# Seven-product pairs one slot later, and seven products in the last pass of a squared-ReLU MLP

## The chip, the cores and the metric

The kernel runs on one core of one Trainium2 chip. A core has a matmul engine (TensorE, PE in the profile, with its weight loads as PEld), three engines for elementwise work (VectorE or DVE, ScalarE or ACT, GpSimdE or POOL), an engine that issues DMAs (SyncE, SP), an on-chip memory of 128 partitions (SBUF), and eight banks of accumulators (PSUM) into which PE writes. The metric is the device time of one execution in microseconds, as the median of several runs. The kernel before took 2000.79 us, the median of 3 runs between 1999.85 and 2004.03.

## The reference, cut to what matters

A two-layer decoder trunk on 256 rows of width 2048, in float32. Layer 0 mixes with a short gated convolution, layer 1 with multi-head latent attention, and each layer ends in a squared-ReLU MLP with 8192 hidden columns. Every sublayer is followed by a normalisation of `ALPHA * h + f(h)`.

```
def sq_relu_mlp(x, w1, w2):
    return jnp.square(jax.nn.relu(x @ w1)) @ w2

for layer in range(DEPTH):                       # DEPTH = 2
    ...                                          # mix: convolution or attention
    h = layer_norm(ALPHA * h + mix, ln_g[layer, 0], ln_b[layer, 0])
    h = layer_norm(ALPHA * h + sq_relu_mlp(h, mlp_w1[layer], mlp_w2[layer]),
                   ln_g[layer, 1], ln_b[layer, 1])
```

x is 256 x 2048, w1 is 2048 x 8192 and w2 is 8192 x 2048 for each layer. The two MLPs take more than half of the time, and the change lies in them.

## The kernel before, in words

**Precision.** A float32 matrix is held as two parts, `hi` (rounded by a cast on ACT, L136) and `lo` (the rest, a subtraction on DVE, L137), and a product is built from two or three matmuls: hi times hi, hi times lo, lo times hi. The function `split` does both steps. `dot` (L309, L311, L312) issues the three matmuls of a 128 x 512 output, and the units of w1 use L224 and L228. Every weight is loaded from memory as a raw tile of 512 KB (`load_raw`, L147, on SP's queue) and split this way before PE can use it. Raw tiles and split tiles come from pools of fixed size, and weights are prepared in the order of one list, `stream`.

**The passes of an MLP.** The 8192 hidden columns are handled in NQ = 8 passes of QC = 8 chunks of 128 columns. For each chunk m of a pass a unit computes `x @ w1` for it: 32 matmuls into one PSUM bank, which `whole` evacuates with a copy on ACT (L366) and an addition on DVE (L367) into half of the tile `fp`. Two chunks share one `fp`, and the pool holds one of them. Relu and square follow on ACT (L732, in one case on DVE, L728).

Passes 0 and 7 multiply the activations by w2 in the ordinary way (`down`, or `down_late` for the last blocks): per output block of 512 columns and half of the rows, three matmuls for each chunk. Passes 1 to 6, called FAST, use a scheme of seven products in place of eight for a 2 x 2 split (`FACTORS`): from a pair of chunks `form` makes sums and differences of quarter tiles (L644 to L648), `split` makes hi and lo of them (tiles h1c, h1a, h3c, h3a), and `fast_products` issues seven dots, 21 matmuls, for one pair of chunks and one pair of output blocks (a group g). A pass has eight such products, numbered i = 0 to 7: four chunk pairs j by two groups. Their w2 tiles (`w2f`) need sums of weights as well, done on DVE (L171, L175, L178) between the casts.

**The sums of a group** lie in seven PSUM banks while the group is being worked on; the eighth bank, "unit", takes the units of w1. When the group is changed (after product i = 3 of a pass; two passes that follow one another take the groups in opposite order, so that none is due between them) the seven banks are copied to SBUF (`put_back`, L620) and those of the other group are copied in (`resume`, L693). After the last fast pass `fold` adds the seven sums to the output blocks (L628).

**Order.** `steps` yields for every pass q and slot m a unit and, from SHIFT = 5 slots behind it, the product that goes with it. So product i of a pass runs at slot i + 5: the first three in its own pass, the other five in the next. After the unit of each odd m, `finish_pair` forms and splits that pair; the first pair of a pass is split after the product of slot m = 1. [...]

**The end.** In the last MLP, `last_sum` copies output blocks into PSUM banks, the last pass's w2 is multiplied there, and `to_out` normalises each row half t: statistics per block (L1042), their aggregate (L1048), a correction by matmuls (L1071, L1076), and scaled outputs (L1059) stored to memory.

Of the kernel before, what the change touches and what calls it, by code (L numbers as in the profile page):

```python
# [11 lines left out]
F32R = mybir.dt.float32r  # L12
AF = mybir.ActivationFunctionType
# [3 lines left out]
P = 128  # L17
W = 256 + 2
T = 256
# [15 lines left out]
NB = 4  # L35
BW = D // NB
FAST = range(1, NQ - 1)
SHIFT = 5


def TURN(q, m, extra):
    return m == 0 or not (q == 1 and m < SHIFT or q == NQ - 1 and m > SHIFT) or extra and q == 1 and m <= NB
FIRST = (0, 1, 2, 3, 4, 6, 8, 12, 16)
LEAD = 4
HEAD = 4
# [11 lines left out]
def trunk(ctx: ExitStack, tc: tile.TileContext, xT, vecs, lead, w_first, w_in, w_out, w_kv, w_q, w_uk, w_uv,  # L57
# [21 lines left out]
    def halves(w):  # L79

        lead = len(w.shape) - 2
        return [(w,)] if lead == 0 else [h for i in range(w.shape[0]) for h in halves(w[i])]
# [6 lines left out]
    def steps():  # L89

        for q in range(1, NQ):
            for m in range(QC):
                p, i = (q, m - SHIFT) if m >= SHIFT else (q - 1, m + QC - SHIFT)
                yield q, m, (p, i // NB, i % NB, (p % 2) ^ (i // NB)) if p in FAST else None

    def mlp_stream(l):
        out = halves(w1[l, :QC]) + halves(w2[l, 0])
        for q, m, pair in steps():
            out += halves(w1[l, q * QC + m])
# [3 lines left out]
        return out + halves(w2[l, NQ - 1])  # L103

    stream += mlp_stream(0) + halves(w_kv) + halves(w_q)
    for g in range(4):
# [27 lines left out]
    def split(hi, lo, src):  # L134

        nc.scalar.copy(hi, src)  # L136
        nc.vector.tensor_tensor(lo, src, hi.bitcast(F32), ALU.subtract)  # L137
# [218 lines left out]
    def fast_products(ps, x, j, fresh, ready, onto=()):  # L356

        b, = take(1, 6)
        a = {n: [x[j // 2][:, j % 2, o, i * P:(i + 1) * P] for o in range(2)] for i, n in enumerate(LEFT)}
        for p, l, r in FACTORS:  # L360
            dot(ps[p], b[r], a[l], p in fresh, p in ready, onto=p in onto)

# [223 lines left out]
    def mlp(idx, ln, blocks, fast, begin=None, extra=None, last=False):  # L586
# [35 lines left out]
        def fold(g):  # L622
# [59 lines left out]
        factors = [act.tile([P, QC // 4, 2, 7 * P], F32R, tag=tag, name=f"h{idx}{tag}") for tag in ("c", "a2")]  # L682
        ps, onto, fresh = {}, set(), set()
        folds = iter(())

# [8 lines left out]
                onto.add(p)  # L694

        begun = {0: FAST[0], 1: FAST[0]}

        def products_of(p, i, j, g):
# [12 lines left out]
            if p == FAST[-1] and j == NB - 1:  # L711
                folds = chain(folds, fold(g))

        for q, m, pair in steps():
            lone = pair is None
            if q == FAST[0] and m == SHIFT:
                for o, _, _ in FACTORS:
                    resume(o, 1)
            w = take(2, 7)
            at = "6" if lone and m % 2 == 0 else "unit"  # L720
            un = psum("ps_u", bank[at])
            mm_run([(w, un)], xhl, 0, NC, NC, turned=TURNED if TURN(q, m, extra) else None)
            if m % 2 == 0:
                u = fast.tile([P, 8 * P], F32, tag="fp", name="fp")
            whole(un, u[:, (m % 2) * T:(m % 2 + 1) * T])
            late = q in FAST and m >= QC - 2
            if late and m % 2:
                nc.vector.scalar_tensor_tensor(u[:, T:2 * T], u[:, T:2 * T], 0.0, u[:, T:2 * T], ALU.max, ALU.mult)  # L728
            elif late or m % 2:
                for function in (AF.Relu, AF.Square):  # L730
                    at = u[:, :T] if late else u[:, :2 * T]
                    nc.scalar.activation(at, at, function)  # L732
            if m % 2 and (m > 1 or lone):
                finish_pair(m // 2, u)
            if extra and q == FAST[0] and m < NB:
                for t in range(2):
                    extra(block, m, t, spare[1 + (2 * m + t) % 3])
            if begin and q == FAST[0] and m < 4:
                if m % 2 == 0:
                    nc.gpsimd.dma_start(parked[:, 4 * m:4 * m + 8, :], held_x[0][:, 4 * m:4 * m + 8, :])  # L740
            if q == FAST[0] and m == SHIFT:
                sums = act.tile([P, 4, 2, BW], F32, tag="xres", name=f"sums{idx}")
            if q == NQ - 1:
                for _ in range(3 if m >= SHIFT else 2):
# [5 lines left out]
            if q == NQ - 1 and last and m >= QC - 2:  # L750
                for t in range(2):
                    last_sum(m - QC + 2, t, spare[2 * (m - QC + 2) + t])
# [273 lines left out]
    def to_out(block, finals, h):  # L1026
# [11 lines left out]
        def scratch(i):  # L1038
            return raws.tile([P, 1024], F32, tag="raw", name=f"u{i}")[:, :BW]

        def finished(n, t, ps):
            nc.vector.bn_stats(out=stats[:, t, n, :], in_=ps)  # L1042
            if n < NB - 1:
# [4 lines left out]
            nc.vector.bn_aggr(out=mv, in_=stats[:, t, :, :])  # L1048
            ve = small.tile([P, 2], F32, tag="ve", name="ve")[:, :1]
            nc.vector.tensor_scalar(ve, mv[:, 1:2], LN_EPS, None, ALU.add)  # L1050
            r = small.tile([P, 2], F32, tag="rr", name="rr")[:, :1]
            us = {}

            def centred(i):
                us[i] = scratch(i)
                nc.vector.scalar_tensor_tensor(us[i], finals[i, t], mv[:, 0:1], gbt[:, i, :BW], ALU.subtract, ALU.mult)

            def scaled(i, x, other, op=ALU.add):
                nc.vector.scalar_tensor_tensor(block(i, t), x, r, other, ALU.mult, op)  # L1059
                store(t, i)  # L1060

            if t == 0:
                rsqrt(r, ve)
                for i in range(NB):
# [5 lines left out]
            for i in range(n):  # L1070
                nc.tensor.matmul(finals[i, t], means, gbt[:, i, :BW], start=False, stop=i > 0, skip_group_check=True)  # L1071
# [4 lines left out]
            nc.tensor.matmul(finals[0, t], devs, gbt[:, 0, BW:], start=False, stop=True, skip_group_check=True)  # L1076
            scaled(n, us[n], gbt[:, n, BW:])
            for i in range(1, n):
                scaled(i, finals[i, t], gbt[:, i, BW:])
            nc.scalar.activation(block(0, t), finals[0, t], AF.Copy, scale=r)  # L1080
            store(t, 0)
# [102 lines left out]
```

## Time and profile before

The profiled execution took 2002.59 us, its span is 2000.7 us, and the mean granted clock of TensorE was 0.998.

| engine | busy, us | share of the span | instructions |
|---|---|---|---|
| PE (matmul) | 1988.5 | 99% | 11062 |
| DVE | 1720.3 | 86% | 2505 |
| ACT | 1289.0 | 64% | 1914 |
| POOL | 5.6 | 0% | 27 |

The page's groups for the work around the change are: the low parts of the weights (L137, 710 of 128 x 1024, 854.6 us), the casts of the weights (L136, 710, 732.5 us), and the units' matmuls (L224, 1792 of 512 columns, 621.2 us; L228, 1792 of 256 columns, 485.0 us).

A line of the timeline gives start and duration in microseconds, engine, line of the kernel, operation, output and inputs, and in brackets how long the engine was idle before it and what released it. A row of a table by stretch gives the span, the busy time of PE, PEld, DVE, ACT and POOL with instruction counts, the granted clock of PE, the DMA share and GB/s; a table asked for one engine has that engine alone.

### The profile page before, as it was taken

The numbers are of one execution on the slowest core, as the hardware profiler recorded it, in microseconds if no ns is written. First come the engines' busy times: TensorE is split into PE (matmuls) and PEld (weight loads), VectorE is DVE, ScalarE is ACT, GpSimd is POOL, SyncE is SP. The second block draws the span as 40 slices with busy tenths as digits, with TensorE's granted clock in tenths as the row PEclk, the third lists the DMA queues.
The fourth block names the chain that finished last, engine by engine and source line by source line (L and its number), as shares of the span: only waits on it lengthen the run. The fifth ranks groups of instructions, "written<-read, shape, count | busy, mean of one in ns | idle before, by whom it ended". The sixth has DMA issues, their size and how long they took to land.

```text
span 2000.7 us, 29698 instructions
## 1 busy us (share of the span) xinstructions
PE 1988.5 (99%) x11062; PEld 1732.5 (87%) x11062; DVE 1720.3 (86%) x2505; ACT 1289.0 (64%) x1914; POOL 5.6 (0%) x27
## 2 busy tenths in 40 slices
PE   9999999999999999999999999999999999999998
PEld 8888888988788888888889998898888888888886
DVE  8667667787899999999988988778889999999995
ACT  6444445586667777677756665558666776767772
POOL 0000000000000000000000000000000000000000
PEclk9999999999999999999999999999999999999999
DMA  9766666574565555665764643656456556565572
GB/s 339 213 190 189 189 189 190 182 238 143 180 215 191 200 194 196 210 205 204 246 223 153 184 144 106 211 182 196 140 194 216 170 203 216 180 212 197 205 267 96
DMA packets 107712, 390.00 MB, mean 195 GB/s; under 512 B 11952, under 2 KB 12720, under 8 KB 107056
## 3 DMA queue, kind: packets, MB, share of 16 engines
q1 hardware_dynamic: 106560, 383.79, 58.7%
q0 software_dynamic: 864, 4.19, 0.6%
q8 instruction: 86, 1.41, 0.3%
q14 instruction: 58, 0.48, 0.1%
q10 hardware_dynamic: 144, 0.13, 0.0%
HBM read 383.87 MB, written 4.19 MB: 194 GB/s over the span
## 4 chain that ended last, share of the span: by engine, by line
PE 95%; DMA 2%; DVE 1%; issue 1%; ACT 0%; SPq 0%; DVEq 0%; POOLq 0%; ACTq 0%
PE ps_u L224 20%; PE ps_l L224 13%; PE ps_u L228 10%; PE ps L312 7%; PE ps L311 7%; PE ps L309 7%; PE ps_l L228 7%; PE ps_d L312 2%; PE ps_d L309 2%; PE ps_d L311 2%; PE ps_w L258 2%; PE ps_w L257 2%; PE ps_w L256 2%; DMA raw<-in_w2f_dram 1%; PE ps_g L258 1%; PE ps_g L256 1%
## 5 line engine op out<-in xcount | busy, mean ns | idle before, releaser
L137 DVE TENSOR_TENSOR lo<-raw,hi 128x1024 fp32r<-128x1024 f32 x710 | 854.6, 1218 | 167.1 <-ACT hi L136 97.6
L136 ACT CAST hi<-raw 128x1024 fp32r<-128x1024 f32 x710 | 732.5, 1054 | 220.2 <-PE ps_l L224 102.2
L224 PE MATMUL ps_u<-xhl,hi 128*128 128x512 f32 x1792 | 621.2, 393 | 0.0
L228 PE MATMUL ps_u<-xhl,lo 128*128 128x256 f32 x1792 | 485.0, 280 | 0.0
L224 PEld LDWEIGHTS ps_u<-xhl,hi 128*128 128x128 f32 x1792 | 328.8, 187 | 67.5 <-DVE fp L367 0.9
L228 PEld LDWEIGHTS ps_u<-xhl,lo 128*128 128x128 f32 x1792 | 338.1, 189 | 12.9
L224 PE MATMUL ps_l<-xhl_a,hi 128*128 128x512 f32 x704 | 244.1, 393 | 0.0
L228 PE MATMUL ps_l<-xhl_a,lo 128*128 128x256 f32 x704 | 195.4, 279 | 0.0
L136 ACT CAST hi_t<-raw_t 128x1024 fp32r<-128x1024 f32 x96 | 101.5, 1057 | 120.4 <-DVE raw_t L171 115.4
L224 PEld LDWEIGHTS ps_l<-xhl_a,hi 128*128 128x128 f32 x704 | 132.1, 188 | 29.9
L228 PEld LDWEIGHTS ps_l<-xhl_a,lo 128*128 128x128 f32 x704 | 131.9, 188 | 0.2
L171 DVE TENSOR_TENSOR raw_t<-raw,raw 128x1024 f32<-128x1024 f32 x96 | 116.9, 1217 | 9.8 <-DMA raw<-in_w2f_dram 9.8
L137 DVE TENSOR_TENSOR lo_t<-raw_t,hi_t 128x1024 fp32r<-128x1024 f32 x96 | 116.9, 1218 | 2.1 <-ACT hi_t L136 1.7
L366 ACT COPY t<-ps_u 128x256 f32<-128x256 f32 x112 | 41.7, 372 | 95.0 <-PE ps_u L228 94.7
L224 PE MATMUL ps_l<-z,hi 128*128 128x512 f32 x240 | 82.4, 391 | 0.0
L258 PE MATMUL ps_w<-xd,hi 128*128 128x258 f32 x256 | 72.7, 284 | 0.0
L256 PE MATMUL ps_w<-xd,hi 128*128 128x258 f32 x256 | 72.3, 282 | 0.0
L257 PE MATMUL ps_w<-xd,lo 128*128 128x258 f32 x256 | 72.3, 282 | 0.0
L224 PE MATMUL ps_l<-oT,hi 128*128 128x512 f32 x208 | 71.3, 391 | 0.0
L732 ACT ACTIVATE fp<-fp 128x512 f32<-128x512 f32 (+1 forms) x112 | 65.9, 588 | 7.2 <-DVE fp L367 6.8
L178 DVE TENSOR_TENSOR raw<-raw 128x512 f32<-128x512 f32 x96 | 66.1, 688 | 2.0
L175 DVE TENSOR_TENSOR raw<-raw,raw_t 128x512 f32<-128x512 f32 x96 | 65.6, 683 | 0.8
(350 smaller groups left out, 3880.0 us busy)
## 6 DMA issues: line engine op xcount, KB each, us to landing
raw<-in_w_dram SPq DMA_DIRECT2D x320, 512.0 KB, 4.1
raw<-in_w2f_dram SPq DMA_DIRECT2D x192, 512.0 KB, 5.2
raw<-in_w_in_dram SPq DMA_DIRECT2D x88, 512.0 KB, 3.7
raw<-in_w_out_dram SPq DMA_DIRECT2D x32, 512.0 KB, 3.7
raw<-in_w_o_dram SPq DMA_DIRECT2D x32, 512.0 KB, 4.2
raw<-in_w_kv_dram SPq DMA_DIRECT2D x10, 512.0 KB, 4.6
raw<-in_w_q_dram SPq DMA_DIRECT2D x8, 512.0 KB, 4.0
raw<-in_w_uk_dram SPq DMA_DIRECT2D x8, 512.0 KB, 4.6
```

The costliest lines, as they stand in the source:

```text
L136: nc.scalar.copy(hi, src)
L137: nc.vector.tensor_tensor(lo, src, hi.bitcast(F32), ALU.subtract)
L171: nc.vector.tensor_tensor(t.rearrange(two, a=2), b12.unsqueeze(1).to_broadcast([P, 2, BW]), r1.rearrange(two, a=2), ALU.subtract)
L178: nc.vector.tensor_tensor(t4, b21, b12, ALU.subtract)
L224: nc.tensor.matmul(ps, w[blk // 8][0][:, blk % 8, :], x, start=first, stop=False)
L228: nc.tensor.matmul(ps[:, :T], w[blk // 8][1][:, blk % 8, :], x[:, :T], start=False, stop=last)
L256: nc.tensor.matmul(ps[:, :W], hi, x[k][:, :W], start=k == 0, stop=False)
L257: nc.tensor.matmul(ps[:, :W], lo, x[k][:, :W], start=False, stop=False)
L258: nc.tensor.matmul(ps[:, :W], hi, x[k][:, W:], start=False, stop=k == NC - 1)
L309: nc.tensor.matmul(ps, x[0], w[0], start=first, stop=False, skip_group_check=onto)
L311: nc.tensor.matmul(ps[:, at], x[0], w[1][:, at], start=False, stop=False, skip_group_check=onto)
L312: nc.tensor.matmul(ps, x[1], w[0], start=False, stop=last, skip_group_check=onto)
```

## The change

- SHIFT goes from 5 to 6: every product runs one slot later behind the units, so two products of a pass run in its own pass and six in the next. Pass 1 has one more slot with a unit alone.
- The first two pairs of a pass are split after the products of slots 2 and 3 (dictionary `rows`), where they were split after the product of slot 1 and after the unit of slot 3.
- In the last MLP, `steps` goes on past the last pass. Two of the four output blocks (group 1, blocks 2 and 3) take the last pass's w2 by four times seven products, two of them in slots 6 and 7 and two behind the units. For that the last pass forms and splits all four pairs. `put_back` is then called for four of the seven sums, and `fold_last` folds the sums into three PSUM banks and one output block; blocks 0 and 1 keep the ordinary way. The order of blocks in `to_out` becomes 2, 3, 0, 1.
- In the first MLP's last pass the late units are split one by one.
- The factor tiles are 8 quarter tiles wide (7 before); `TURN` loses its clause on `extra`, which ran some units of the last MLP's pass 1 with their matmuls in another order (`TURNED`).

```
-SHIFT = 5
+SHIFT = 6
...
-def TURN(q, m, extra):
-    return m == 0 or not (...) or extra and q == 1 and m <= NB
+def TURN(q, m):
+    return m == 0 or not (q == 1 and m < SHIFT or q == NQ - 1 and m > SHIFT)
...
-        for q in range(1, NQ):
-            for m in range(QC):
+        for q in range(1, NQ + 1):
+            for m in range(QC if q < NQ else SHIFT):
...
+        def fold_last(g):
+            s1, s5, s7, s6 = (sums[:, i, g, :] for i in range(4))
+            left, right = 2 * g, 2 * g + 1
+            finals.update({(left, 1): ps["2"], (right, 1): ps["3"], (left, 0): ps["4"], (right, 0): block(right, 0)})
+            for d, a, b in ((ps["2"], ps["2"], s1), (s6, s6, s1), (ps["3"], ps["3"], s6), (s7, s7, s6),
+                            (ps["4"], ps["4"], s7), (block(right, 0), block(right, 0), s7), (ps["3"], ps["3"], s5),
+                            (block(right, 0), block(right, 0), s5)):
+                nc.vector.tensor_tensor(d, a, b, ALU.add)
...
-            if q in FAST:
+            if q in FAST or last:
                 form(u)
-                split(f[:, 0, :], f[:, 1, :], u[:, P:])
+                at = slice(P if q in FAST else 0, 8 * P)
+                split(f[:, 0, at], f[:, 1, at], u[:, at])
...
-            end = i == 0 or p == FAST[-1]
+            end = i == 0 or p == FAST[-1] and not last
...
                 for o in order:
+                    if p == NQ - 1:
+                        if o in OWN:
+                            put_back(o, g, ps[o])
+                        continue
...
-            late = q in FAST and m >= QC - 2
+            late = m >= QC - 2
...
-            if m % 2 and (m > 1 or lone):
-                finish_pair(m // 2, u)
+            if late and q not in FAST and not last:
+                f, at = factors[m // 4][:, 1], slice(m % 2 * T, (m % 2 + 1) * T)
+                split(f[:, 0, at], f[:, 1, at], u[:, at])
+            else:
+                rows[m // 2] = u
+            if m % 2 and (m > 3 or lone) and m // 2 in rows:
+                finish_pair(m // 2, rows.pop(m // 2))
...
-            if m == 1 and not lone:
-                finish_pair(0, u)
+            if m in (2, 3) and not lone:
+                finish_pair(m - 2, rows.pop(m - 2))
...
-            for i, (n, t) in enumerate(((2, 0), (3, 0), (2, 1), (3, 1))):
-                last_sum(n, t, spare[4 + i])
-            blocks(block, finals, h)
+            for n, t, o in ((0, 0, "unit"), (1, 0, "1"), (0, 1, "5"), (1, 1, "7")):
+                last_sum(n, t, bank[o])
+            blocks(block, finals, h, lambda: fold_last(1))
...
+        order = (2, 3, 0, 1)
...
-        for n in range(2):
-            down(h, finished, n, finals)
-        down_late(h, finished, range(2, NB), finals)
+        fold_last()
+        for n in order[:2]:
+            for t in range(2):
+                finished(n, t, finals[n, t])
+        down_late(h, finished, order[2:], finals)
```

More of the change, by code (lines that the diff above doesn't have):

```diff
@@ L37 @@
 FAST = range(1, NQ - 1)
-SHIFT = 5
-def TURN(q, m, extra):
-    return m == 0 or not (q == 1 and m < SHIFT or q == NQ - 1 and m > SHIFT) or extra and q == 1 and m <= NB
+SHIFT = 6
+def TURN(q, m):
+    return m == 0 or not (q == 1 and m < SHIFT or q == NQ - 1 and m > SHIFT)
 FIRST = (0, 1, 2, 3, 4, 6, 8, 12, 16)
@@ L87, in trunk, with steps @@
     stream += halves(w_out)
-    def steps():
-        for q in range(1, NQ):
-            for m in range(QC):
+    def steps(last):
+        for q in range(1, NQ + 1):
+            for m in range(QC if q < NQ else SHIFT):
                 p, i = (q, m - SHIFT) if m >= SHIFT else (q - 1, m + QC - SHIFT)
-                yield q, m, (p, i // NB, i % NB, (p % 2) ^ (i // NB)) if p in FAST else None
+                pair = (p, i // NB, i % NB, (p % 2) ^ (i // NB)) if p in FAST or last and p == NQ - 1 and i < NB else None
+                if q < NQ or pair:
+                    yield q, m, pair
     def mlp_stream(l):
         out = halves(w1[l, :QC]) + halves(w2[l, 0])
-        for q, m, pair in steps():
-            out += halves(w1[l, q * QC + m])
+        for q, m, pair in steps(l == 1):
+            if q < NQ:
+                out += halves(w1[l, q * QC + m])
             if pair:
@@ L102, in mlp_stream @@
                 out.append((w2f[l, p, g, j, 0], w2f[l, p, g, j, 1]))
-        return out + halves(w2[l, NQ - 1])
+        return out + halves(w2[l, NQ - 1, :2] if l else w2[l, NQ - 1])
     stream += mlp_stream(0) + halves(w_kv) + halves(w_q)
@@ L358, in fast_products @@
         b, = take(1, 6)
-        a = {n: [x[j // 2][:, j % 2, o, i * P:(i + 1) * P] for o in range(2)] for i, n in enumerate(LEFT)}
+        a = {n: [x[j // 2][:, j % 2, o, i * P:(i + 1) * P] for o in range(2)] for i, n in enumerate(LEFT, 1)}
         for p, l, r in FACTORS:
@@ L681, in mlp @@
         spare = [bank[p] for p in ("3", "1", "5", "7", "2", "4", "6", "unit")]
-        factors = [act.tile([P, QC // 4, 2, 7 * P], F32R, tag=tag, name=f"h{idx}{tag}") for tag in ("c", "a2")]
+        factors = [act.tile([P, QC // 4, 2, 8 * P], F32R, tag=tag, name=f"h{idx}{tag}") for tag in ("c", "a2")]
         ps, onto, fresh = {}, set(), set()
@@ L696, in mlp @@
         begun = {0: FAST[0], 1: FAST[0]}
+        rows = {}
         def products_of(p, i, j, g):
@@ L710, in products_of @@
                         resume(o, 1 - g)
-            if p == FAST[-1] and j == NB - 1:
+            if p == FAST[-1] and j == NB - 1 and end:
                 folds = chain(folds, fold(g))
-        for q, m, pair in steps():
+        for q, m, pair in steps(last):
             lone = pair is None
+            if q == NQ:
+                products_of(*pair)
+                continue
             if q == FAST[0] and m == SHIFT:
@@ L719, in mlp @@
             w = take(2, 7)
-            at = "6" if lone and m % 2 == 0 else "unit"
+            at = "6" if lone and (m - SHIFT) % 2 else "unit"
             un = psum("ps_u", bank[at])
-            mm_run([(w, un)], xhl, 0, NC, NC, turned=TURNED if TURN(q, m, extra) else None)
+            mm_run([(w, un)], xhl, 0, NC, NC, turned=TURNED if TURN(q, m) else None)
             if m % 2 == 0:
@@ L743, in mlp @@
             if q == NQ - 1:
-                for _ in range(3 if m >= SHIFT else 2):
+                for _ in range(3 if m >= SHIFT else 2 if not last or m > 2 else 0):
                     next(folds, None)
@@ L747, in mlp @@
                 products_of(*pair)
-            if m == 1 and not lone:
-                finish_pair(0, u)
-            if q == NQ - 1 and last and m >= QC - 2:
-                for t in range(2):
-                    last_sum(m - QC + 2, t, spare[2 * (m - QC + 2) + t])
+            if m in (2, 3) and not lone:
+                finish_pair(m - 2, rows.pop(m - 2))
         for _ in folds:
@@ L1024, in turn_residual, with to_out @@
         nc.vector.scalar_tensor_tensor(block(n, t), ps, ALPHA, block(n, t), ALU.mult, ALU.add)
-    def to_out(block, finals, h):
+    def to_out(block, finals, h, fold_last):
         gbt = act.tile([P, NB, 2 * BW], F32, tag="b", name="gbt")
@@ L1039, in scratch @@
             return raws.tile([P, 1024], F32, tag="raw", name=f"u{i}")[:, :BW]
+        order = (2, 3, 0, 1)
         def finished(n, t, ps):
             nc.vector.bn_stats(out=stats[:, t, n, :], in_=ps)
-            if n < NB - 1:
+            if n != order[-1]:
                 if t == 1:
@@ L1063, in finished @@
                 rsqrt(r, ve)
-                for i in range(NB):
+                for i in order:
                     centred(i)
@@ L1069, in finished @@
             nc.scalar.activation(means, negative, AF.Copy, scale=mv[:, 0:1])
-            for i in range(n):
-                nc.tensor.matmul(finals[i, t], means, gbt[:, i, :BW], start=False, stop=i > 0, skip_group_check=True)
+            one = order[0]
+            for i in order[:-1]:
+                nc.tensor.matmul(finals[i, t], means, gbt[:, i, :BW], start=False, stop=i != one, skip_group_check=True)
             rsqrt(r, ve, lambda: centred(n))
@@ L1075, in finished @@
             nc.scalar.activation(devs, id_t, AF.Copy, scale=ve)
-            nc.tensor.matmul(finals[0, t], devs, gbt[:, 0, BW:], start=False, stop=True, skip_group_check=True)
+            nc.tensor.matmul(finals[one, t], devs, gbt[:, one, BW:], start=False, stop=True, skip_group_check=True)
             scaled(n, us[n], gbt[:, n, BW:])
-            for i in range(1, n):
+            for i in order[1:-1]:
                 scaled(i, finals[i, t], gbt[:, i, BW:])
-            nc.scalar.activation(block(0, t), finals[0, t], AF.Copy, scale=r)
-            store(t, 0)
-        for n in range(2):
-            down(h, finished, n, finals)
-        down_late(h, finished, range(2, NB), finals)
+            nc.scalar.activation(block(one, t), finals[one, t], AF.Copy, scale=r)
+            store(t, one)
+        fold_last()
[3 more added lines that the diff above has]
+        down_late(h, finished, order[2:], finals)
     with tc.tile_pool(name="fast2", bufs=1) as fast:
```

## The prediction

> **What bounds the kernel now.** I read the page first, for the engine that ends last; then tables by stretch around the steps that the diff moves; then the timeline of single instructions there.
>
> ```profile
> PE 1988.5 (99%) x11062; PEld 1732.5 (87%) x11062; DVE 1720.3 (86%) x2505; ACT 1289.0 (64%) x1914; POOL 5.6 (0%) x27
> PE 95%; DMA 2%; DVE 1%; issue 1%; ACT 0%; SPq 0%; DVEq 0%; POOLq 0%; ACTq 0%
> ```
>
> TensorE holds 95% of the chain that ended last: time falls only where it has fewer matmuls or fewer waits. VectorE at 86% is a mean. In the steps of the seven-product passes it is full (table by stretch, last MLP, next to the last pass):
>
> ```profile
> 1900.80:1911.10 10.30, 10.30 (x56) 8.72 (x55) 10.30 (x14) 6.80 (x11) 0.00 (x0) 1.00 0.70 226
> 1911.10:1922.00 10.90, 10.90 (x58) 9.27 (x57) 10.90 (x15) 7.25 (x11) 0.00 (x0) 1.00 0.57 194
> ```
>
> After the span stand PE, PEld, DVE, ACT, POOL, the granted clock and DMA. PE and DVE are both busy throughout, so a stall of one soon becomes one of the other. PE's few stalls sit in the first seven-product pass of each MLP (product i=3):
>
> ```profile
> 501.57:511.94 10.37, 10.37 (x54) 8.74 (x53) 8.40 (x11) 6.66 (x9) 0.00 (x0) 1.00 0.49 155
> 511.94:518.48 6.54, 5.81 (x33) 4.80 (x32) 6.07 (x9) 1.55 (x3) 0.00 (x0) 1.00 0.87 308
> 518.48:528.53 10.05, 7.87 (x22) 5.91 (x23) 6.03 (x7) 6.67 (x11) 0.00 (x0) 0.66 0.45 147
> 528.53:538.95 10.42, 10.42 (x55) 8.84 (x54) 8.74 (x10) 10.09 (x15) 0.00 (x0) 1.00 0.42 125
> 1468.39:1474.57 6.18, 5.09 (x23) 3.86 (x22) 5.25 (x7) 4.32 (x9) 0.00 (x0) 1.00 0.50 139
> 1947.40:1990.95 43.55, 43.55 (x194) 1.00 0.32 112
> 1884.55:1889.35 4.80, 4.80 (x23) 1.00 0.61 227
> ```
>
> The first and fourth rows are undisturbed steps of 10.37 us: one W1 unit and one product. A product is 4.80 (last row, 21 matmuls, 0.2286 each), so a unit is 5.57. The stretches between are one unit (6.54) and one product (10.05); 1468.39 is a product of the last MLP. The row of 43.55 is the ordinary output of the last pass, 192 matmuls, 0.2268 each.
>
> ```profile
> 512.84 0.42 DVE L728 SCALAR_TENSOR_TENSOR fp<-fp 128x256 f32<-128x256 f32 x1
> ...
> 514.32 0.28 DVE L645 TENSOR_TENSOR fp<-fp 128x128 f32<-128x128 f32 x1
> ...
> 519.11 1.22 DVE L171 TENSOR_TENSOR raw_t<-raw,raw 128x1024 f32<-128x1024 f32 x1 [1.10 <-DMA raw<-in_w2f_dram]
> 520.26 1.08 DVE L137 TENSOR_TENSOR h1a<-fp,h1a 128x896 fp32r<-128x896 f32 x1
> ```
>
> ```profile
> 518.48 0.50 PE L309 MATMUL ps<-hi,h1a 128*128 128x512 f32 x1 [0.73 <-ACT h1a L136]
> ...
> 521.39 0.79 PE L312 MATMUL ps<-hi,h1a 128*128 128x512 f32 x1 [2.18 <-DVE h1a L137]
> 521.99 0.63 PE L309 MATMUL ps<-hi,h1a 128*128 128x512 f32 x1
> 522.41 0.63 PE L311 MATMUL ps<-lo,h1a 128*128 128x512 f32 x1
> 1471.03 0.73 PE L312 MATMUL ps<-hi,h3a 128*128 128x512 f32 x2 [1.09 <-DVE h3a L137]
> 1011.82 0.50 PE L312 MATMUL ps_d<-hi,h1a 128*128 128x512 f32 x1 [1.20 <-DVE h1a L137]
> ```
>
> Of the DVE rows three belong to the last pair of activations (relu, a small add, the low part of the split at 520.26), and one, ahead of that split, waited for weights, and PE waits for that pair (h1a, h3a). After 0.73 and 2.18 matmuls follow at 0.42 (521.99 to 522.41) instead of 0.23, with the clock at 0.66 over the stretch: of the 6.2 us lost there, 2.9 are waits and 3.3 the slower clock. After 1.09 the clock stayed 1.00.
>
> **What the change takes away.** (1) With SHIFT 6 product i=3 runs one step, 10.37 us, later, more than any of these waits. First MLP: (6.54−5.57)+(10.05−4.80) = 6.22 us. Last MLP: 6.18−4.80 = 1.38. What is late next is the same split one product on, with 10.37−2.9, some 7 us, to spare; if that cover goes, the price is what it is now. (2) At the first MLP's end the wait of 1.20, with the slow matmul beside it (0.50 for 0.39) 1.3, goes: late units are split by halves, and the split stands earlier on DVE's queue. (3) The last MLP's last pass computes two of its four output blocks by seven products: 84 matmuls for 96, so 96×0.2268+84×0.2286 = 40.98 for 43.55, a gain of 2.57. Together 11.5.
>
> DMA issues on SP's queue are as many as before, each product's weights one unit later in the stream and one unit later needed; POOL's queue is not touched. The longer factor tiles and their wider split (1024 for 896 columns, four pairs in the last pass) cost DVE and ACT 0.1 each; I put 0.4 in sum, range 0 to 0.6. Fewer turned units in the last MLP: ±0.3, taken as 0.
>
> **What it adds, first: the change of group (after product i=3, now in slot m=1) and the two slots behind it.** The activations of m=0 and 1 lie in one buffer, fp (one copy). They are now split after the product at m=2, where before it was after that at m=1. So the evacuation of unit m=2, which writes the next fp, must stand behind that split, the split behind product i=4, which still reads the factors it overwrites, and unit m=3 behind the evacuation, since all units of a pass use one PSUM bank. [...] Both queues around this place in the trace (last MLP, ACT then DVE):
>
> ```profile
> 1884.79 0.37 ACT L366 COPY t<-ps_u 128x256 f32<-128x256 f32 x1 [2.40 <-PE ps_u L228]
> 1886.11 0.59 ACT L693 COPY ps<-acc 128x512 f32<-128x512 f32 x1
> 1886.64 0.58 ACT L620 COPY sums<-ps 128x512 f32<-128x512 f32 x1
> 1887.12 1.05 ACT L136 CAST hi_t<-raw_t 128x1024 fp32r<-128x1024 f32 x1
> 1888.06 1.06 ACT L136 CAST hi<-raw 128x1024 fp32r<-128x1024 f32 x1
> ...
> 1901.04 0.64 ACT L732 ACTIVATE fp<-fp 128x512 f32<-128x512 f32 x1
> 1901.58 1.04 ACT L136 CAST hi<-raw 128x1024 fp32r<-128x1024 f32 x1
> ```
>
> ```profile
> 1888.20 1.23 DVE L137 TENSOR_TENSOR lo_t<-raw_t,hi_t 128x1024 fp32r<-128x1024 f32 x1 [0.24 <-ACT hi_t L136]
> 1889.35 1.22 DVE L137 TENSOR_TENSOR lo<-raw,hi 128x1024 fp32r<-128x1024 f32 x1
> 1890.48 0.68 DVE L137 TENSOR_TENSOR t<-raw,t 128x512 fp32r<-128x512 f32 x1
> 1891.08 1.22 DVE L137 TENSOR_TENSOR lo<-raw,hi 128x1024 fp32r<-128x1024 f32 x1
> ...
> 1900.59 0.42 DVE L367 TENSOR_TENSOR fp<-ps_u,t 128x256 f32<-128x256 f32 x1
> ```
>
> Start to start, on ACT: copies 0.48 and 0.53 (0.50), cast 0.95, activation 0.54; on DVE 1024 columns 1.14, 512 columns 0.60; the evacuation lasts 0.42. Count from the end of unit m=1. On ACT the new order has a copy, the first put-back and reload (their sum is ready after 3 matmuls, both done at 2.0), three casts (2.85), two activations (1.08) and a half cast (0.5): 6.5. Then twelve copies of 0.50: 12.5. Then a cast of 1.05: 13.5. Only then can DVE begin, and it goes on without a break: four of 1024 (4.56), one of 512 (0.60), one of 1024 (1.14), the split of the fp (1.0), one of 512 (0.60) and the evacuation (0.42): 8.3, so 21.8. PE has until then the product of m=1, unit m=2, the product of m=2, the next product and two matmuls: 4.80+5.57+4.80+4.80+0.46 = 20.4. It waits 1.4. Between PE and this chain there is no other work: in steady steps DVE is full. Eight such places (q=4 to 7, two MLPs): 11.2. Lower end 0: copies and casts overlap better than their order says. Upper end 1.9: 0.5 more where a weight cast lands before the copies. I take 1.4, since both ends come from the same rows and the sum of pitches lies nearer the upper one.
>
> Queued behind the waiting evacuation on DVE are the low parts of the next weights; behind ACT's cast of the fp, the casts of the next product. Either delays the product after. [...]
>
> **Second: the last pass.** Its product i=3 follows the last unit with only 18 matmuls and one product between: 18×0.2286+4.80 = 8.9 us. Behind that unit stand on DVE, durations less the 0.08 by which neighbours overlap: copy and evacuation (0.37+0.42), three of 512 (1.8), a relu of 256 (0.34), four of 1024 (4.56), adds of 128, 256 and 128 (0.20+0.34+0.20), 8.25, and a fourth 512 (0.6): 8.85. Then ACT, whose cast already under way has 0.9 left, casts the activations (1.05): 10.8. PE waits 1.9; 1.1 if the cast under way went behind, 2.2 with semaphores.
>
> **Third: the tail.** In the built order four scaled outputs of the first row half stand on DVE between the last statistics and their aggregate, where now they run before the last matmul:
>
> ```profile
> 1984.56 2.74 DVE L1059 SCALAR_TENSOR_TENSOR acc<-u,rr,gbt 128x512 f32<-128x512 f32 x4
> ...
> 1991.32 0.70 DVE L1042 BATCH_NORM_STATS2 stats<-ps_e 128x6 f32<-128x512 f32 x1 [2.81 <-PE ps_e L312]
> 1992.05 0.26 DVE L1048 BATCH_NORM_AGGREGATE mv<-stats 128x2 f32<-128x24 f32 x1
> ```
>
> Four take 2.74 less the 0.08 of overlap; nothing covers them there: 2.65. Lower end 0, if the last weights come sooner than the order supposes and the statistics end late; I take 2.65.
>
> **Sum.** −11.5+11.2+1.9+2.65+0.4 = +4.65. The profiled execution took 2002.59 us (span 2000.7); the median of the runs is 2000.79, 1.8 lower, within the runs' own scatter (1999.85 to 2004.03). I start between the two, at 2001.5, and forecast 2006.0 (rounded down). What a measurement of this kernel can tell from no change is 0.2%, 4.0 us: 1996.8 to 2004.8.
>
> **Rivals.** (a) *The swap is covered*, because put-backs and casts come earlier on the chip than pitches along the order make them: waits 0. −11.5+1.9+2.65+0.4 = −6.55: 1994.9, with the tail's lower end 1992.3. For it: the trace shows no PE wait in the change of groups before (1884 to 1905). Against: DVE is full there, and between the two products there is now no unit. It decides below a wait of (11.5−4.7−4.95)/8 = 0.23 a place, 4.7 being the way from 2001.5 to 1996.8. 0.18.
> (b) *Half covered.* Waits of 0.9 a place, 7.2: +0.65, 2002.1, no change. 0.24.
> (c) *The clock.* Where waits add up as at 518 to 521, the slow clock takes up to 3.3 more; at three of the eight changes of group +9.9: 2016.0. Against: the single waits of 1.09 and 1.20 cost one slow matmul at most. 0.10. [...]
> (d) *The stall stays.* If product i=3 of the first MLP comes as late again, 6.2 return: 2012.3. For it: at 519.11 the split stood behind weights that came 1.10 late. Against: 10.37 us more room. 0.08.
>
> **How the numbers follow.** The forecast has 0.40; with (c) and (d) slower has 0.58, same 0.24 from (b), faster 0.18 from (a). The range 1996 to 2013 leaves out most of (a) and the worse part of (c), some 0.2; the forecast's own is 2003 to 2010, by waits of 1.0 to 1.9.
>
> **What would show it.** Right: product i=3 in the first fast pass back to 4.80 at clock 1.00; a PE wait of 1 to 2 us near each change of group in q=4 to 7, released by the evacuation or a cast; 1.9 before the last pass's product i=3; aggregate 2.7 later than the last statistics. Wrong: no PE idle at the changes of group, or a clock under 1.00 there.

## The result, and the profile after

The changed kernel takes 2012.9 us (median of 4 runs, 2012.58 to 2014.15) against 2000.6 of the kernel before: a ratio of 1.0061, with a 95% interval of 1.0045 to 1.0077. It is slower by some 12 us. Its profiled execution took 2012.86 us with a span of 2011.0.

From the page of the changed kernel, its busy times and the chain that ended last:

```profile
PE 1991.4 (99%) x11050; PEld 1726.9 (86%) x11050; DVE 1748.0 (87%) x2540; ACT 1289.4 (64%) x1916; POOL 5.7 (0%) x27
PE 76%; DVE 11%; ACT 10%; issue 3%; DMA 1%; DVEq 0%; ACTq 0%
```

PE has 12 matmuls fewer, is busy 2.9 us longer, and its part of the chain fell from 95% to 76%: VectorE and ScalarE now release it. The summary of PE's waits (what it waited for, total us, times, longest) for the two stretches that hold the MLPs' passes, first MLP and then last:

```profile
PE ps_u L227 <- DVE fp L370: 1.7, 2, 1.0
PE ps L312 <- ACT hi L139: 1.2, 3, 0.5
PE ps L312 <- ACT t L139: 0.9, 2, 0.5
PE ps L314 <- DVE t L140: 0.5, 1, 0.5
...
PE ps L312 <- ACT hi L139: 1.8, 4, 0.5
PE ps L312 <- ACT h3a L139: 1.7, 1, 1.7
PE ps L312 <- ACT t L139: 1.5, 3, 0.5
PE ps_u L227 <- DVE fp L370: 0.8, 1, 0.8
```

The waits for the splits h1a and h3a in the first fast passes, which the prediction showed, are gone; the evacuation (fp), the casts (hi, t) and the low parts (t) are what PE waits for now. Product i=3 of the first fast pass takes 4.80 us at clock 1.00 (21 matmuls; the row counts a neighbour at each end with them):

```profile
522.40:527.20 4.80, 4.80 (x23) 3.95 (x22) 4.32 (x6) 3.88 (x7) 0.00 (x0) 1.00 0.42 130
```

One change of group, PE's timeline and then DVE's (last MLP, q=6):

```profile
1828.31 0.40 PE L315 MATMUL ps<-hi,h3c 128*128 128x512 f32 x1
1829.19 0.50 PE L312 MATMUL ps<-t,h3c 128*128 128x512 f32 x1 [0.48 <-ACT t L139]
1830.14 0.73 PE L312 MATMUL ps<-hi,h3a 128*128 128x512 f32 x2 [0.45 <-ACT hi L139]
1830.83 0.50 PE L314 MATMUL ps<-t,h3c 128*128 128x512 f32 x1
1831.16 0.40 PE L315 MATMUL ps<-t,h3c 128*128 128x512 f32 x1
1831.40 0.39 PE L227 MATMUL ps_u<-xhl,hi 128*128 128x512 f32 x1
```

```profile
1822.79 2.36 DVE L140 TENSOR_TENSOR lo<-raw,hi 128x1024 fp32r<-128x1024 f32 x2 [3.22 <-ACT hi L139]
1825.07 1.22 DVE L140 TENSOR_TENSOR lo_t<-raw_t,hi_t 128x1024 fp32r<-128x1024 f32 x1
1826.21 1.22 DVE L140 TENSOR_TENSOR lo<-raw,hi 128x1024 fp32r<-128x1024 f32 x1
1827.35 0.68 DVE L181 TENSOR_TENSOR raw<-raw 128x512 f32<-128x512 f32 x1
1827.95 1.22 DVE L140 TENSOR_TENSOR lo<-raw,hi 128x1024 fp32r<-128x1024 f32 x1
1829.08 1.08 DVE L140 TENSOR_TENSOR h3c<-fp,h3c 128x896 fp32r<-128x896 f32 x1
1830.09 0.69 DVE L140 TENSOR_TENSOR t<-raw,t 128x512 fp32r<-128x512 f32 x1
1830.69 0.42 DVE L370 TENSOR_TENSOR fp<-ps_u,t 128x256 f32<-128x256 f32 x1
```

DVE's row is the predicted one, instruction for instruction: it begins after 3.22 us of waiting for ACT and takes 8.3 us without a break, 1822.79 to 1831.11. PE meets the chain a little ahead of the evacuation: its two waits end with casts of the next weights on ACT (t and hi), and when unit m=3 begins at 1831.40 the evacuation is just over. PE's seven starts span 3.09 us for six matmuls that take 1.37 at 0.229: 1.72 are lost. Measured this way (start to start, above the pace of the matmuls), the first MLP loses 0.93 (q=2), 0.80 (q=4), 1.66, 1.69 and 2.39 (q=7), the last one 1.04, 0.99, 1.69, 1.72 and 1.85 at the same places: 14.8 us. At q=3 nothing is lost.

The last pass and the tail, PE and then DVE:

```profile
1969.65 0.50 PE L312 MATMUL ps<-hi,h3a 128*128 128x512 f32 x1 [1.70 <-ACT h3a L139]
...
2000.58 3.78 PE L1098 MATMUL ps<-gbt,umeans 128*128 128x512 f32 x4 [4.10 <-ACT umeans L1095]
```

```profile
1996.52 0.70 DVE L1068 BATCH_NORM_STATS2 stats<-ps_e 128x6 f32<-128x512 f32 x1 [0.21 <-PE ps_e L315]
1997.13 2.72 DVE L1085 SCALAR_TENSOR_TENSOR acc<-u,rr,gbt 128x512 f32<-128x512 f32 x4
1999.77 0.26 DVE L1074 BATCH_NORM_AGGREGATE mv<-stats 128x2 f32<-128x24 f32 x1
```

The four scaled outputs stand ahead of the aggregate, as foreseen. What follows was not. The table by stretch of the tail, kernel before and then after (span, busy PE, PEld, DVE, ACT, POOL, granted clock):

```profile
1990.90:1992.87 1.97, 0.39 (x3) 0.01 (x1) 1.48 (x4) 0.46 (x2) 0.00 (x0) 1.00 0.00 0
1992.87:1996.60 3.73, 3.69 (x8) 1.43 (x8) 3.09 (x8) 0.73 (x3) 0.00 (x0) 1.00 0.21 81
```

```profile
1996.10:2000.58 4.48, 0.38 (x2) 0.00 (x1) 4.23 (x10) 0.45 (x2) 0.00 (x0) 0.82 0.43 154
2000.58:2006.85 6.27, 6.27 (x8) 2.38 (x8) 3.10 (x8) 0.74 (x3) 0.00 (x0) 0.58 0.39 141
```

The wait grew from 1.97 to 4.48 us, and the correction behind it (eight matmuls in the trace, two for each of the four in the program) took 6.27 in place of 3.73, at a granted clock of 0.58 instead of 1.00. From the last product to the end it is 9.8 us before and 14.9 after.

### The profile page after: what moved, and what is told of

Same layout as the page of the kernel before. It is cut to its first block, busy times and chain, and to the rows that moved or that the text cites. A ratio compares the mean times of both kernels' runs of the same rounds, so it can differ in the third digit from the quotient of the medians.

```text
span 2011.0 us, 29715 instructions
## 1 busy us (share of the span) xinstructions
PE 1991.4 (99%) x11050; PEld 1726.9 (86%) x11050; DVE 1748.0 (87%) x2540; ACT 1289.4 (64%) x1916; POOL 5.7 (0%) x27
## 4 chain that ended last, share of the span: by engine, by line
PE 76%; DVE 11%; ACT 10%; issue 3%; DMA 1%; DVEq 0%; ACTq 0%
PE ps_u L227 14%; PE ps_l L227 13%; PE ps_u L231 7%; PE ps_l L231 7%; DVE lo L140 4%; ACT hi L139 4%; PE ps L312 4%; PE ps L314 4%; PE ps L315 4%; PE ps_d L314 2%; PE ps_d L315 2%; PE ps_d L312 2%; PE ps_w L261 2%; PE ps_w L260 2%; PE ps_w L259 2%
## 5 line engine op out<-in xcount | busy, mean ns | idle before, releaser
L139 ACT CAST hi_t<-raw_t 128x1024 fp32r<-128x1024 f32 x100 | 105.8, 1058 | 200.1 <-DVE raw_t L174 193.7
L140 DVE TENSOR_TENSOR lo_t<-raw_t,hi_t 128x1024 fp32r<-128x1024 f32 x100 | 122.0, 1220 | 5.2 <-ACT hi_t L139 4.9
L174 DVE TENSOR_TENSOR raw_t<-raw,raw 128x1024 f32<-128x1024 f32 x100 | 122.0, 1220 | 3.4 <-DMA raw<-in_w2f_dram 3.4
```

The source lines that it names most:

```text
L174: nc.vector.tensor_tensor(t.rearrange(two, a=2), b12.unsqueeze(1).to_broadcast([P, 2, BW]), r1.rearrange(two, a=2), ALU.subtract)
```

## The experiments

The kernel before had between 2000.6 and 2001.0 us as its median in each group of runs below.

**1. The shift alone.** The last MLP's last pass stays the ordinary one; `TURN` is that of the change.

```
-SHIFT = 5
+SHIFT = 6
...
+                rows[m // 2] = u
+            if m % 2 and (m > 3 or lone) and m // 2 in rows:
+                finish_pair(m // 2, rows.pop(m // 2))
...
-            if m == 1 and not lone:
-                finish_pair(0, u)
+            if m in (2, 3) and not lone:
+                finish_pair(m - 2, rows.pop(m - 2))
```

> Only the shift by one slot (SHIFT 6, the first two pairs split after the products of slots 2 and 3, late units of the first MLP split singly); the last MLP's last pass is the ordinary one with 192 matmuls. My theory: it saves the stalls of the first fast passes and of the first MLP's end (6.2+1.4+1.3 = 8.9 us) and pays the waits behind the changes of group, which sum to some 14.9 us in the changed kernel's profile; +6.0: 2006.6 us (2004 to 2009). The tail is that of the kernel before. Rival, that the new last pass is what costs: 2001 or less.

Measured: 2010.65 us, ratio 1.0049 (1.0037 to 1.0062), so the shift by itself costs some 9.7 us. The waits at the changes of group are there (8.1 us in the first MLP and 7.9 in the last, 2.4 of each in its last pass), and the tail takes 9.8 us, as before. The shift is what costs most. The expected +6.0 was 3.7 too low: 1.1 of it are these waits (16.0 in place of 14.9), and 1.3 the gain, which had been read from an execution of the kernel before that was slower than most (experiment 5); the rest is open, and the five executions lie between 2008.76 and 2013.74.

**2. A second buffer.** Units m=2 and 3 of a fast pass are evacuated into two tiles that lie idle in the passes (the next normalisation's sums, now allocated at first use, and the last one's scales). The sums of quarters are then four instructions in place of three and the split is two.

```
+            if m % 2 == 0 and m == 2 and q in FAST:
+                pair_u = [act.tile([P, 2 * T], F32, tag=tag, name=f"fp{tag}") for tag in ("ab", "SQ")]
+                u = pair_u[0]
+            elif m % 2 == 0:
+                u = pair_u = fast.tile([P, 8 * P], F32, tag="fp", name="fp")
```

> The changed kernel, with units m=2 and 3 of a fast pass evacuated into a second buffer (two free tiles of 512 columns), so that nothing of theirs waits for the split of the first pair. My theory, that the single buffer between evacuation and late split makes the waits at the changes of group: some 14.9 us of waits go, some 0.6 us for four instructions in place of two come back: 1998.6 us (1996 to 2002). Rival, that VectorE and ScalarE are simply full there (twelve copies and the weights' parts) and the waits only move on by a step: within 3 us of the changed kernel, 2010 to 2014.

Measured: 2005.33 us, ratio to the kernel before 1.0023 (1.0014 to 1.0032): 7.6 us of the 12.3 are gone. PE's waits in the same two stretches:

```profile
PE ps_u L227 <- DVE fp L370: 1.1, 1, 1.1
PE ps L312 <- ACT hi L139: 0.5, 1, 0.5
PE ps_u L227 <- DVE fpab L370: 0.2, 1, 0.2
...
PE ps_u L227 <- DVE fp L370: 1.5, 1, 1.5
PE ps L312 <- ACT h3a L139: 1.2, 1, 1.2
...
PE ps_u L227 <- DVE fpab L370: 0.4, 1, 0.4
```

The places of q=2, 4, 5 and 6 lose next to nothing any more; a wait for the new buffer (fpab) at q=3 costs 0.5 to 0.7. What is left stands in the last passes, where this kernel still has the one buffer (2.4 and 2.9 us), and in the tail. The expectation had counted those two passes among the mended ones. So the single buffer makes the waits of the fast passes; that VectorE is full did not bring them back there.

**3. The tail's order.** The scaled outputs of the first row half are kept in a list and written behind the second half's statistics.

```
-                    scaled(i, us[i], gbt[:, i, BW:])
+                rest.append(lambda: [scaled(i, us[i], gbt[:, i, BW:]) for i in order])
...
+            rest.pop()()
             nc.scalar.activation(ve, ve, AF.Copy, scale=r)
```

> The changed kernel, with the four scaled outputs of the first row half written into the program behind the last statistics; in the built order one of them stands ahead of the aggregate, where four stood. My theory: the aggregate comes 2.0 us earlier, PE's last wait falls from 4.3 to some 2.4 us, and the six matmuls behind it run at 0.43 us each again, for 0.85: 2012.9-2.0-2.5 = 2008.4 us (2007 to 2010). Rival, that the clock falls after 2.4 us of waiting as well: 2010.9.

Measured: 2010.0 us, 2.9 less than the changed kernel. The aggregate came earlier by the 2 us expected; but the clock fell here too, in the middle of the correction:

```profile
1998.71 2.80 PE L1099 MATMUL ps<-gbt,umeans 128*128 128x512 f32 x4 [2.11 <-ACT umeans L1096]
2001.31 1.91 PE L1099 MATMUL ps_e<-gbt,umeans 128*128 128x512 f32 x2
2003.01 1.10 PE L1105 MATMUL ps<-gbt,udevs 128*128 128x512 f32 x2
```

The first two of the matmuls ran at 0.43 us, the last ones at 0.85 (2001.31 to 2003.01 for two). The measured time lies between theory and rival, nearer to the rival: a wait of 2.5 us, start to start, still cost the clock here.

**4. PE kept busy in the tail's wait.** The matmuls added write a bank that is not read any more.

```
+            for _ in range(24):
+                nc.tensor.matmul(finals[order[0], 0][:, :T], h[0][:, 0, :P], h[0][:, 0, :], start=True, stop=True, skip_group_check=True)
             means = scratch("means")[:, :P]
```

> The changed kernel, with 24 matmuls of 256 columns more (2.8 us) behind the last product of the output, into a bank that is not read any more; nothing else moves, and the wait for the means stays. My theory, that the halved clock after 4.3 us of idling makes the six correcting matmuls cost 0.85 us each instead of 0.43: they are back at 0.43, 2010.4 us (2009.5 to 2011.5). Rival, that these matmuls are slow because of their operands in banks filled by VectorE: no change, 2012.9.

Measured: 2010.57 us, 2.3 less with 24 matmuls more. The two stretches that answer to those of the changed kernel:

```profile
1996.56:2001.05 4.49, 3.26 (x27) 3.02 (x25) 4.24 (x10) 0.46 (x2) 0.00 (x0) 1.00 0.42 154
2001.05:2004.50 3.45, 3.45 (x8) 1.43 (x8) 2.91 (x8) 0.73 (x3) 0.00 (x0) 1.00 0.50 180
```

The wait for the means is the same 4.5 us, with PE busy in it, and the correction takes 3.45 us at clock 1.00 where it took 6.27 at 0.58. It was the clock, and not the operands.

**5. The kernel before, profiled again.**

> The kernel before once more, for a second profile of it. The first profile's execution (2002.59 us) was slower than the median of the others (2000.9 of 15). If the halved clock behind product i=3 of the first fast pass (3.3 us of the 6.2) depends on when the waits fall, this profile may show the wait of some 3 us without it, at some 2000 us; if it belongs to every execution, 6.2 us are lost there again.

Measured: 2000.95 us; this profiled execution took 2000.99, which is the median. The stretch of product i=3 of the first fast pass, and PE there:

```profile
516.88:525.50 8.62, 5.66 (x19) 4.02 (x18) 6.62 (x8) 6.50 (x11) 0.00 (x0) 0.80 0.33 101
```

```profile
520.85 0.80 PE L312 MATMUL ps<-hi,h1a 128*128 128x512 f32 x1 [2.17 <-DVE h1a L137]
...
523.87 0.40 PE L309 MATMUL ps<-hi_t,h1a 128*128 128x512 f32 x1
```

The wait is as long as in the first profile, but the slow clock ends after some six matmuls, at 523.7, where it lasted for some twelve there: 4.8 us are lost, against 6.1 counted the same way. It is a part of the scatter between runs: over 23 of the 33 other executions of this group the mean granted clock is 0.999, as in this profile, over two it is 0.998, as in the first one, and over eight 1.000. The first profile had drawn the dear end of it.

**6. The last pass alone**, with SHIFT 5 and the old places of the splits.

```
-SHIFT = 6
+SHIFT = 5
...
-            if m in (2, 3) and not lone:
-                finish_pair(m - 2, rows.pop(m - 2))
+            if m == 1 and not lone:
+                finish_pair(0, rows.pop(0))
```

> Only the new last pass (two output blocks by seven products, sums folded in PSUM, new order of blocks), with the products five slots behind as before. My theory: 2.6 us of matmuls saved; product i=3 of the last pass then has 33 matmuls (7.5 us) between itself and the last unit instead of 8.9, so some 3.3 us of wait, and the clock may halve there (0 to 3); no waits behind the changes of group, since the first pair is split in the slot before; the tail is that of the kernel before plus the four scaled outputs ahead of the last statistics: 2001.0-2.6+3.3 = 2001.7, to 2005 with the clock. Rival, that the changed kernel's tail belongs to the last pass: 2.65+2.4 more, 2006.8.

Measured: 2005.34 us, ratio 1.0024 (1.0015 to 1.0033): 4.6 us slower than the kernel before for 12 matmuls fewer. The longer of the two waits ahead of product i=3, and the stretches behind that wait and in the tail:

```profile
1963.74 0.50 PE L314 MATMUL ps_e<-lo,h3c 128*128 128x512 f32 x1 [2.14 <-DVE lo L140]
```

```profile
1963.74:1970.00 6.26, 6.25 (x26) 4.63 (x26) 6.26 (x8) 3.74 (x4) 0.00 (x0) 1.00 0.93 255
...
1990.46:1993.70 3.24, 0.39 (x2) 0.00 (x1) 3.17 (x7) 0.45 (x2) 0.00 (x0) 0.89 0.81 285
1993.70:2000.00 6.30, 6.30 (x8) 2.52 (x8) 3.16 (x8) 0.73 (x3) 0.00 (x0) 0.51 0.27 103
```

The waits in the pass sum to 3.2 us (start to start), as expected, though on the weights of the ordinary blocks, and the clock behind them stayed at 1.00; the tail with its slow clock comes with the last pass, as the rival had it: 14.1 us from the last product to the end. The two halves of the change are nearly additive: 9.7 and 4.6, together 14.3, against 12.3 measured on the whole; some 1.2 of the difference are the waits of this pass, 3.2 here and 1.97 in the changed kernel.

**7. All mended.** The second buffer in every pass, the tail's order of experiment 3 and ten matmuls without use.

```
-            if m % 2 == 0 and m == 2 and q in FAST:
+            if m % 2 == 0 and m == 2 and q:
...
+            for _ in range(10):
```

> The changed kernel with the second buffer in every pass (the last too), the aggregate ahead of three of the scaled outputs, and 10 matmuls without use behind the last product. If the waits of the last passes (2.4 and 3.1 us) have the same cause as the others, they go: 2005.3-5.0; the tail gives 2.0+2.4 back: 1996 us (1994 to 1999), under the kernel before. Rival, that a full VectorE brings the waits back elsewhere in the last pass: 2000 or more.

Measured: 2004.24 us, ratio 1.0019 (1.0010 to 1.0028). Two new waits took the gain. One is at the first MLP's end, where PE now comes before the reloaded residual (2.7 us, see the next run). The other is product i=3 of the last pass:

```profile
1958.25:1962.72 4.47, 0.39 (x2) 0.00 (x0) 4.47 (x9) 2.99 (x4) 0.00 (x0) 1.00 1.03 414
1962.72:1969.00 6.28, 6.28 (x21) 5.03 (x21) 5.14 (x6) 4.08 (x6) 0.00 (x0) 0.73 0.88 312
```

VectorE is busy for all of the 4.47 us in which PE waits, and afterwards the clock is at 0.73. In the last pass the rival had it right, as far as this trace shows: VectorE is full, and what PE does not wait for at the change of group it waits for here. No run took work off VectorE there to test it.

**8. The shift alone with the second buffer in every pass.**

> The shift by one slot alone (ordinary last pass), with the second buffer in every pass: only its gain, without its waits. Theory: 2010.7 less some 14 us of waits: 1996.5 us (1995 to 1999). Against the kernel with all mended the difference is the new last pass alone: 2.6 us of matmuls less its 1.4 to 1.9 us of wait, so within 2 us of it. Rival, that the stall of the first fast pass was no loss in the usual execution: 1999 to 2001.

Measured: 1998.51 us, ratio 0.9989 (0.9980 to 0.9998). The edit is that of experiment 2 on the kernel of experiment 1, with `and q` as in 7. In its profile the first MLP's end is new:

```profile
1011.44 1.22 PE L420 MATMUL mu0p<-xback,ones 128*128 128x256 f32 x2 [3.25 <-DVE xback L418]
```

```profile
1007.80:1011.44 3.64, 0.39 (x2) 0.00 (x0) 0.34 (x2) 1.04 (x1) 0.13 (x1) 0.85 0.98 371
1011.44:1017.20 5.76, 5.76 (x14) 4.51 (x15) 5.76 (x12) 0.37 (x1) 0.41 (x1) 0.50 0.98 380
```

The reload of the residual can only start when the last fold has freed its tile, and PE now arrives 3.4 us before it has landed; then it works at half the clock for 5.8 us. Experiment 7, which adds to this kernel the new last pass, with the tail's order and the ten matmuls, takes 5.7 us longer; in experiment 6 the new last pass cost 4.6. Both times it was a loss, though it has 12 matmuls fewer.

**9. The second buffer in the fast passes and in the last MLP's last pass only**, on the shift alone.

```
-            if m % 2 == 0 and m == 2 and q:
+            if m % 2 == 0 and m == 2 and (q in FAST or last and q):
```

> The shift alone with the second buffer in the fast passes and in the last MLP's last pass, not in the first MLP's last pass. There PE came to the first MLP's end too early in the run before: 3.4 us of wait for the reloaded residual and some 2.7 us of halved clock. Theory: the 2.4 us of waits in that pass come back, the 6.1 go, 1998.5-3.7 = 1994.8 us (1993 to 1997). Rival, that PE is early there anyway and still waits for the reload: 1998 to 2000.

Measured: 1997.87 us (1997.31 to 1998.84), ratio 0.9986 (0.9977 to 0.9995), the lowest median of all and 3.0 us under the kernel before; the 1994.8 expected was missed. In the profile the wait of 3.4 us and the slow clock behind it are gone, the waits of that pass (2.4 us) are back, and the span is 1996.0 for 2000.7. In the medians the difference is 0.6 us only, less than the scatter of experiment 8: its profiled execution was the slowest of its eleven (2002.48), which is where I had the price from. The granted clock of the executions tells how often such a price is paid: in experiment 8 it is 0.998 or 0.999 over the five slowest (1999.55 to 2002.48) and 1.000 over the other six (1996.10 to 1998.51), among them the median; in experiment 9 it is 1.000 over nine of eleven. That it fell at this place in all five is not shown.

## Why the prediction was right or wrong

The direction was right, and the time lay inside the range, at its upper end: 2012.9 for 2006.0, a loss of 12 us for the 4.65 of the sum, and outside the 2003 to 2010 that the forecast's own waits gave. The number alone would have spoken for rival (d), the stall that stays (2012.3); that is a coincidence, since the stall had gone. The three places of loss were the ones named, and the chain, the order on VectorE and the wait of the last pass came about as described. Three terms of the sum were off in size, and they make up the difference.

- **The stall of the first fast pass.** It went, as predicted: in the changed kernel the 42 us around that place ran without a gap at clock 1.00, and product i=3 took its 4.80. But it was worth 6.2 us only in the execution that was read; in the one at the median it is 4.8 (experiment 5). The term was 1.3 too large. The two smaller gains were right: PE's waits at the first MLP's end and in the last MLP's first fast pass are absent after.
- **The change of group.** The chain from the put-backs to the evacuation came out as counted (8.3 us on DVE, experiment 2 for its cause). The 1.4 a place supposes that every engine keeps to its built order and that nothing passes the waiting evacuation; that was an assumption of mine, and no run shows the 1.4 itself. In its place the trace shows the nine instructions of DVE at q=6 in the foreseen order, 44 matmuls on PE between units m=2 and 3 from q=4 on, and these losses. At q=5 and 6, where the sum had 1.4, it is 1.66 to 1.72; at q=4 it is 0.8 to 1.0, at q=7 1.85 and 2.39. So the eight places of the sum cost 12.8 for 11.2, with errors of both signs. The other 2.0 are the two places at q=2, which the sum put at nothing: it counted q=4 to 7 alone, and gave no reason for leaving out q=2 and 3. There PE has 37 or 38 matmuls between units m=2 and 3, where it has 44 later, so it comes to the evacuation sooner; it waited at q=2 and not at q=3. In sum 14.8 for 11.2: 3.6 too small.
- **The last pass.** 1.9 was predicted for the wait of product i=3, and 1.97 measured (start to start, with the first matmuls behind it).
- **The tail.** The wait was right: 4.48 us for 1.97, 2.5 more. The step that failed is the one that put nothing behind it: that the clock is lower behind the wait (0.58 over the correction) was not weighed, since the rival on the clock spoke of the changes of group alone. It is 2.5 us more (6.27 for 3.73), and experiment 4 shows that it is the clock; so the tail lost 5.1 for 2.65.
- **Rival (c)** was wrong where it was put: at none of the changes of group did the clock fall (it is 1.00 from 452 to 1000 us and from 1400 to 1975), though waits of 0.6 to 1.1 us followed each other there.

Together 1.3+3.6+2.5 = 7.4 us, and 4.65+7.4 is the 12 measured. The stretches of the two profiles say the same: against experiment 5 the one from the first fast pass to the first MLP's end is 1.1 us longer (561.3 for 560.2), that of the last MLP 5.7 (596.5 for 590.8), the tail 5.1; in sum 11.9, the whole difference of the two spans (2011.0 for 1999.1). For the lesser edits this leaves a few tenths, where 0.4 stood.

Not every wait was followed by the slow clock. In the changed kernel's tail, where PE waits 4.3 us, the clock fell 2.6 us into the wait, and in experiment 3 a wait of 2.3 us was enough; on the other side the 2.4 us of experiment 6 and the 2.7 of experiment 7's first wait left the clock at 1.00. Between 2 and 3 us, then, the length alone did not decide.

What did can be read from the traces. In the profiles of the two kernels and of experiments 3 and 5 to 8, behind the first 7 us, a slow clock that ended before the kernel did lasted 3.41 us (experiments 3, 5 and 7) or 6.83 (the kernel before, the changed kernel, experiment 8 and the tail of experiment 6), and the changes of the clock lie whole multiples of 3.413 us apart (in the kernel before at 520.32, 527.14 and 2001.70, in the changed kernel at 1998.96, 2005.79 and 2009.20). When a profile is cut into stretches of 3.41 us at these places, the clock fell at the end of the stretches in which PE had stood still for 2.2 us or more, by an estimate from the starts of its matmuls and their pace (2.2 in the kernel before and 2.8 in experiment 5 at the first stall; 2.6 in the changed kernel's tail; 2.3 in experiment 3, 2.4 in experiment 7, 2.3 in experiment 8), and it did not fall at the end of the others: up to the last matmul the most of these is 1.4 us in the kernel before and 1.7 in the changed kernel, and experiment 7's first wait has 2.0. Experiment 3, where PE was back at 1998.71:

```profile
1996.33:1999.74 3.41, 1.30 (x5) 0.55 (x4) 3.19 (x10) 0.60 (x2) 0.00 (x0) 1.00 0.22 85
1999.74:2003.15 3.41, 3.41 (x6) 1.35 (x5) 2.83 (x7) 0.70 (x2) 0.00 (x0) 0.50 0.66 257
```

The waits that left the clock alone lie across such a border: with all that PE stood still there, experiment 6 has 1.5 us in one stretch and 1.6 in the next, experiment 7 has 1.1 and 2.0. Where a wait falls thus counted beside its length in these profiles, and the borders do not lie at the same times in every execution (1998.96 in the changed kernel's tail, 1999.74 in experiment 3's). This is read from the profiles; no run moved a wait to test it.

## What to carry to other kernels

When a step is moved by a slot, look at every buffer whose last reader moves with it: a single buffer between an evacuation and a late reader turns one slot of slack into a wait at each turn, and a second one, of 4 KB per partition, took 7.6 us off the changed kernel here. Fewer matmuls on the full engine are no gain by themselves: the new last pass saved 12 and cost time each time it was tried. A term read from a disturbed stretch, a slow clock above all, should be checked against a second profile of the same kernel. And a wait on TensorE has two prices: its length, and, where some 2.2 us of it fall into one stretch of 3.41 us, as in these traces, the slower matmuls behind it (2.5 us in the changed kernel's tail). So a sum should have a term for both.

## What had not been expected of the hardware

After a wait of 2.3 us (beyond the usual pace) between the last product and the correction, the first two matmuls still ran at full speed (0.43 us) and the following ones at half (0.85, experiment 3); 24 matmuls without use in the wait kept the clock at 1.00 and were worth 2.3 us (experiment 4). The same wait of the same kernel was followed by some twelve slow matmuls in one execution (6.83 us of halved clock) and some six in another (3.41 us).
